# A hybrid decoder trunk: token halves for three pairs, seven products for eight

## The chip, the cores and the metric

The kernel runs on one core of a Trainium2 chip. The metric is the device time of one execution in microseconds. The engines are named as in the profile: PE (TensorE, matmuls), PEld (its weight loads), DVE (VectorE), ACT (ScalarE), POOL (GpSimd) and SP (SyncE, which here only issues DMAs).

## The reference

The input is x, 512 tokens of 1024 float32 values. Two layers follow, and a final RMSNorm. Layer 0 has a causal Conformer convolution and a SwiGLU FFN; layer 1 has sliding-window attention with its own query and output projections over one shared K/V, and a SwiGLU FFN. D_FF is 2816.

```python
def swiglu_ffn(x, w_up, w_down):
    gate, up = jnp.split(x @ w_up, 2, axis=-1)
    return (jax.nn.silu(gate) * up) @ w_down

def conformer_conv(x, w_pw1, b_pw1, w_dw, b_dw, ln_g, ln_b, w_pw2, b_pw2):
    a = jax.nn.glu(x @ w_pw1 + b_pw1, axis=-1)
    y = lax.conv_general_dilated(a, w_dw[:, None, :], ...) + b_dw
    y = jax.nn.silu(layernorm(y, ln_g, ln_b))
    return y @ w_pw2 + b_pw2
...
    for l in range(DEPTH):
        if l < N_A_LAYERS:
            h = h + conformer_conv(rmsnorm(h, norm_mix[l]), ...)
        else:
            ...
            h = h + attn @ w_o[j]
        h = h + swiglu_ffn(rmsnorm(h, norm_ffn[l]), ffn_w_up[l], ffn_w_down[l])
    return rmsnorm(h, norm_final)
```

## The kernel before

Everything lies transposed: h is [channels, tokens], 8 tiles of 128 channels by 512 tokens. Most matmuls keep float32 accuracy by splitting both operands into a high part (rounded to the fast format fp32r) and a low part (the rest): mm3 issues high × high, high × low and low × high (lines 380 to 382), the weights being the stationary operand. mm2 (lines 412 and 413) is the same for the second token half in the "twin" form, where one moving operand of 512 columns holds the high and the low part of 256 tokens side by side. A few chunks are multiplied as plain float32 (line 378).

The weights come as chunks of 512 KB, in the order of a list, PLAN. SP loads a chunk into one of six raw buffers, up to nine chunks ahead; ACT rounds it to the high part whi (L294), DVE subtracts to get the low part wlo (L297), each with four buffers and up to three chunks ahead of PE. The order of the instructions on every engine is fixed at build time by a scheduler, from the order of the code, and from rules of the kernel's own: issue_after (an instruction is not placed ahead of another), job and pace (background work is advanced at given chunk counts), and rate.

A "pair" is two 128-channel tiles of D_FF with gate and up; there are 11 pairs. In layer 0 the FFN treats them in two ways (HALVES0):

- Pairs 0 to 3 "by token halves": for the first half of the tokens (right after the first half of the convolution) four up chunks per pair, the gate, and two down chunks per pair, and later the same for the second half in the twin form.
- Pairs 4 to 10 "by seven products": the 2 × 2 block product of weights (channel blocks) and tokens (halves) is done with seven block products instead of eight, as in Strassen's scheme (SEVEN: A11 B11, S1 T1, S2 T2, A12 B21, S3 T3, S4 B22, A22 T4). S1 to S4 are sums of weight blocks. They are made in DRAM by DMAs: copy_sums has SP copy one block, and prepare() has POOL issue an accumulating DMA that adds the other (L289). share[0] is the number of such steps per weight chunk. T1 to T4 are sums of the tokens' rows, made by Rows0.sums.

The stages of layer 0, in the order of time: the convolution of the first token half; its second projection pw2 and the FFN of that half with pairs 0 to 3, with the convolution of the second half on DVE, ACT and POOL in the background (Half.background: the taps, then sums and scales for the LayerNorm, then spread and rows); the A12 products of pairs 4, 5 and 6, which need only tokens of the first half (FIRST); pw2 of the second half; the twin FFN of the second half; the seven products of pairs 4 to 10; their down chunks, at 512 columns.

The LayerNorm's last steps set when pw2 of the second half can start. spread is one matmul (L1089) that broadcasts mean and scale over the partitions; from it DVE makes the rows of z (L1101, L1102), ACT applies silu (L1103) and rounds (L544), and DVE subtracts for the low part (L545). In SevenPair.take, the bank of product A11 is read by DVE (L830) before product S2 writes into it; L840, L842, L849, L850 and L853 belong to the pair's other evacuations and its gate. The twin FFN's result goes through ACT (L604), DVE (L605), POOL (L606) and DVE (L607) into h.

Of the kernel before, what the change touches and what calls it, by code (L numbers as in the profile page):

```python
# [11 lines left out]
F32 = mybir.dt.float32  # L12
# [6 lines left out]
P = 128  # L19
# [12 lines left out]
EPS = 1e-6  # L32
NEG = -1e30
N_WARM = 6
HALVES0 = ((0, 4), (4, 11))
FIRST = (4, 5, 6)
LAST = FT // 2 - 1
STEPS1 = [("up", 0), ("up", 1), ("up", 2), ("low", 0)]
for _p in range(3, LAST, 2):
# [32 lines left out]
    return [(kind, pair, n.split()[0]) for n in SEVEN]  # L72


def part2_products():

    steps, held = [], []
    for pair in range(*HALVES0[1]):
        names = [n.split()[0] for n in SEVEN]
        if pair in FIRST:  # L80
            names = ["A11", "S1", "S2", "S4", "S3", "A22"]
        steps += [(pair, names[0])] + held
        held = [(pair, names.pop())] if pair in FIRST else []
        steps += [(pair, n) for n in names[1:]]
    return steps + held
# [6 lines left out]
def chunk_plan():  # L92
    plan = []

    def pw2():
        for g in range(2):
            for kp in range(KT // 2):
                plan.append(("pw2", kp, g))

    def downs(lo, hi):  # L100
        for g in range(2):
            for kp in range(lo, hi):
                plan.append(("down", 0, kp, g))
# [24 lines left out]
    return plan  # L128
# [81 lines left out]
def hybrid_trunk(ctx: ExitStack, tc: tile.TileContext, xT, W, prm_in, wdw_in, sinks, relb, onehot, fin, lead, out):  # L210
# [151 lines left out]
    def get(*key):  # L362
# [10 lines left out]
        sh = dict(a=n)  # L373
        return tuple(w and w.rearrange("p (a b) -> p a b", **sh) for w in (hi, lo))

    def mm3(out, w, x, start, stop, **kw):
        if w[1] is None:
            nc.tensor.matmul(out, w[0], x, start=start, stop=stop)  # L378
            return
        nc.tensor.matmul(out, w[0], x[0], start=start, stop=False, **kw)  # L380
        nc.tensor.matmul(out, w[0], x[1], start=False, stop=False, **kw)  # L381
        nc.tensor.matmul(out, w[1], x[0], start=False, stop=stop, **kw)  # L382

    class Act:
        def __init__(self, n, w=512):
# [177 lines left out]
    def down_group(keys, act_of, banks, on_step=None, on_m=None):  # L563
        nk = len(keys)
        w = banks[0].shape[-1]
        for ci, (key, kts) in enumerate(keys):
# [14 lines left out]
            if on_step is not None and on_m is None and ci == nk - 1:  # L581
                on_step()
                on_step()

    def ffn_part(layer, part, xg, tok, rms, on_h=None, twin=False, plain=None):
        lo, hi = HALVES0[part]
        hid = ffn_up(layer, lo, hi, xg, tok, rms, twin, plain)
        w = tok.stop - tok.start
        for g in range(2):
# [27 lines left out]
            if w == 256:  # L617
                rs_bc = rms.step2().unsqueeze(1).to_broadcast([P, 2, w])
                for e, b in enumerate(full):
                    i = g * 4 + 2 * e  # L620
                    nc.vector.tensor_mul(b, b, rs_bc)
                    nc.vector.tensor_add(hT[:, i:i + 2, tok], b, hT[:, i:i + 2, tok])
                    for k in range(2 if on_h is not None else 0):
                        on_h(i + k)
                continue
            for m in range(4):
                t = h[g * 4 + m][:, tok]
# [298 lines left out]
    def norm_x(rms, tok, pb=None):  # L926
# [4 lines left out]
                                           op0=ALU.mult, op1=ALU.mult)  # L931
        return pb

    with tc.tile_pool(name="conv", bufs=2) as cv:
        a_pad = [cv.tile([P, PAD + S], F32, tag=f"apad{ct}", name=uid("apad"), bufs=1) for ct in range(KT)]
        for a in a_pad:
# [39 lines left out]
        class Half:  # L976
# [131 lines left out]
            def background(self):  # L1108

                gen = self.conv()  # L1110
                due = []
                for p in range(KT // 2):
                    for s in range(TAPS - N_POOL[self.hf][p] + 1):
                        next(gen)
                        while due and due[0][0] <= s:
                            due.pop(0)[1]()
                        yield
                    due = [(10, self.shift_rows)] if p == 0 else []
                    due += [(11, lambda p=p: self.squares(p)), (12, lambda p=p: self.adds(p)), (15, lambda p=p: self.sums(p))]
# [132 lines left out]
        first = {pair: first[:, n, :].rearrange("p (a s) -> p a s", a=2) for n, pair in enumerate(FIRST)}  # L1252
        for pair in FIRST:
            pace()
            r = new_chain()
            product(("up0", pair, "A12"), [[x0["ffn0"][4 + k][e][:, HALF[0]] for k in range(4)] for e in range(2)], r, True)
            nc.scalar.copy(first[pair], r)
        flush()

# [12 lines left out]
    class Rows0:  # L1272
# [11 lines left out]
        def sums(self):  # L1284
# [6 lines left out]
            for n, (name, t, f, a, b) in enumerate((  # L1291
# [5 lines left out]
                if n == 3:  # L1297
# [6 lines left out]
                both = z0.tile([P, 2, 4, 256], F32R, tag="z0", name=uid("rows"), bufs=5)  # L1304
# [5 lines left out]
    z0 = part2.enter_context(tc.tile_pool(name="part2", bufs=5))  # L1310
    plain1 = z0.tile([P, KT, W2], F32, tag="z0", name=uid("plain1"), bufs=5)
# [12 lines left out]
    lo0, hi0 = HALVES0[1]  # L1324
    hid0, open_pairs = [], {}
    left = [n for n, _ in part2_products()]
    for pair, a in part2_products():
        if pair not in open_pairs:
            c = z0.tile([P, 2, 2, 2, 256], F32, tag="z0", name=uid("up"), bufs=5)
            open_pairs[pair] = SevenPair("up0", pair, rows0, c, first.get(pair))  # L1330
        open_pairs[pair].take(a)
        left.remove(pair)
        if pair in left:
            continue
        c = open_pairs[pair].gates()
        if 2 * (pair - lo0) == len(hid0):
            if pair == hi0 - 1:
                q = quad()
                two = q[:, 0:2], q[:, 2:4]
            else:  # L1340
                two = quad(), quad()
            hid0 += [[d[:, k, :] for d in two] for k in range(two[0].shape[1])]
        for m in range(2):
            split([d.rearrange("p (s q) -> p s q", s=2) for d in hid0[2 * (pair - lo0) + m]], c[:, m, :, 0, :])
    part2.close()

    attn = ExitStack()
    at = attn.enter_context(tc.tile_pool(name="attn", bufs=2))
    job(chain(*(read_bias(*b) for b in ((0, 0), (0, 1), (1, 0)))), (seen[0], 0), (seen[0] + 10, 7))
    share[0] = 0.6  # L1350
    if True:
# [346 lines left out]
```

## Time and profile before

| what | value |
|---|---|
| time, median of 3 runs | 1043.3 us (1042.69 to 1043.46) |
| the profiled execution | 1043.27 us, span 1041.5 us |
| granted TensorE clock | 0.997 |
| PE busy | 1031.5 us (99%), 6580 instructions |
| DVE busy | 776.5 us (75%) |
| ACT busy | 613.0 us (59%) |
| POOL busy | 473.2 us (45%) |
| DMA | 248.33 MB, mean 238 GB/s |

Matmuls are pipelined: a row's duration overlaps the next row's, and what a matmul costs PE is the step from its start to the start of the next. The stages before lie at these times of the span: pw2 of the first half from about 129 us, FFN of the first half 158 to 234, three A12 products 235 to 244, pw2 of the second half 244 to 267, twin FFN 267 to 335, seven products 335 to about 464, downs to about 540.

### The profile page before, as it was taken

Reading aid. Unit: us, or ns where it says so; the run is one execution under the profiler, and the core shown is the slowest. Engines: PE = TensorE matmul, PEld = TensorE weight load, DVE = VectorE, ACT = ScalarE, POOL = GpSimd, SP = SyncE. Lnnn points to the kernel's source line nnn. Section 1 sums busy time; section 2 is a strip of 40 time slices with the busy share of each in tenths; the row PEclk is TensorE's granted clock in tenths of the full one; section 3 lists DMA queues with packets and bytes.
Section 4 is the critical chain, followed back from the end, with each engine's and each line's share of the span. In section 5 each row is a group of like instructions: output and inputs, shape, how many; then the busy total and the mean of one; then the engine's idle time right before and its main releaser. Section 6 shows DMA issues by size and latency. Waiting matters only on the chain.

```text
span 1041.5 us, 17709 instructions
## 1 busy us (share of the span) xinstructions
PE 1031.5 (99%) x6580; PEld 932.6 (90%) x6580; DVE 776.5 (75%) x1202; ACT 613.0 (59%) x1062; POOL 473.2 (45%) x569
## 2 busy tenths in 40 slices
PE   9999999999999999999999999999999999999996
PEld 8888889999988999998888877788989999898995
DVE  3999989978789777673536566678686877868777
ACT  3887798847776556552333565466655556554654
POOL 3999999930535233221214255405442334434134
PEclk9999999999999999999999999999999999999998
DMA  9999747999999988999969766955879988877742
GB/s 356 340 315 207 205 126 204 272 256 275 249 239 262 304 220 284 256 301 244 286 209 254 210 183 183 228 154 152 252 230 312 287 264 264 245 233 222 224 150 81
DMA packets 67282, 248.33 MB, mean 238 GB/s; under 512 B 7579, under 2 KB 13884, under 8 KB 66364
## 3 DMA queue, kind: packets, MB, share of 16 engines
q1 hardware_dynamic: 54236, 200.75, 55.9%
q0 software_dynamic: 12672, 46.14, 24.8%
q8 instruction: 51, 0.84, 0.3%
q10 hardware_dynamic: 288, 0.31, 0.1%
q14 instruction: 35, 0.29, 0.1%
HBM read 241.93 MB, written 97.52 MB: 326 GB/s over the span
## 4 chain that ended last, share of the span: by engine, by line
PE 98%; DMA 0%; DVE 0%; issue 0%; POOLq 0%; SPq 0%; POOL 0%; ACT 0%
PE bank L380 20%; PE bank L382 20%; PE bank L381 20%; PE bank L960 10%; PE bank L902 9%; PE bank L412 4%; PE bank L378 4%; PE bank L413 2%; PE bank L1441 1%; PE bank L1483 1%; PE bank L1470 1%; PE bank L1058 1%; PE bank L1607 1%; PE bank L948 1%; DMA both<-in_lead_dram 0%; PE bank L1562 0%
## 5 line engine op out<-in xcount | busy, mean ns | idle before, releaser
L297 DVE TENSOR_TENSOR wlo<-raw,whi 128x1024 fp32r<-128x1024 f32 x246 | 329.7, 1348 | 136.8 <-ACT whi L294 136.5
L294 ACT CAST whi<-raw 128x1024 fp32r<-128x1024 f32 x246 | 257.1, 1049 | 276.6 <-PE bank L381 194.1
L380 PE MATMUL bank<-quad,whi 128*128 128x256 f32 (+1 forms) x976 | 307.4, 317 | 0.0
L381 PE MATMUL bank<-quad,whi 128*128 128x256 f32 (+1 forms) x976 | 306.6, 315 | 0.0
L382 PE MATMUL bank<-quad,wlo 128*128 128x256 f32 (+1 forms) x976 | 305.7, 315 | 0.0
L380 PEld LDWEIGHTS bank<-quad,whi 128*128 128x128 f32 x976 | 185.5, 191 | 12.8 <-issue 1.6
L381 PEld LDWEIGHTS bank<-quad,whi 128*128 128x128 f32 x976 | 186.0, 191 | 11.9 <-issue 0.5
L382 PEld LDWEIGHTS bank<-quad,wlo 128*128 128x128 f32 x976 | 185.6, 191 | 11.8 <-issue 0.4
L853 POOL TENSOR_TENSOR up<-up 128x512 f32<-128x512 f32 x34 | 62.9, 1851 | 283.6 <-ACT up L850 283.6
L1002 POOL TENSOR_TENSOR pr<-pr,pr 128x256 f32<-128x256 f32 x208 | 155.4, 788 | 2.6 <-ACT pr L1001 2.5
L380 PE MATMUL bank<-rows,whi 128*128 128x256 f32 x488 | 138.0, 283 | 0.0
L381 PE MATMUL bank<-rows,whi 128*128 128x256 f32 x488 | 137.8, 282 | 0.0
L382 PE MATMUL bank<-rows,wlo 128*128 128x256 f32 x488 | 137.8, 282 | 0.0
L1009 DVE SCALAR_TENSOR_TENSOR bank<-apad,wdw,bank 128x256 f32<-128x256 f32 x248 | 112.4, 485 | 3.4
L1001 ACT ACTIVATE pr<-apad,wdw 128x256 f32<-128x256 f32 x208 | 98.3, 502 | 14.9 <-POOL pr L1002 13.1
L960 PE MATMUL bank<-quad,w 128*128 128x256 f32 x448 | 98.7, 380 | 0.0
L960 PEld LDWEIGHTS bank<-quad,w 128*128 128x128 f32 x448 | 84.9, 190 | 11.8 <-DVE bank L1009 0.2
L380 PEld LDWEIGHTS bank<-rows,whi 128*128 128x128 f32 x488 | 93.1, 191 | 0.3
L381 PEld LDWEIGHTS bank<-rows,whi 128*128 128x128 f32 x488 | 93.1, 191 | 0.3
L382 PEld LDWEIGHTS bank<-rows,wlo 128*128 128x128 f32 x488 | 93.0, 191 | 0.0
L491 POOL TENSOR_TENSOR tmp<-tmp,tmp 128x256 f32<-128x256 f32 (+1 forms) x28 | 26.8, 957 | 101.4 <-ACT tmp L487 96.2
L412 PE MATMUL bank<-quad,whi 128*128 128x512 f32 x168 | 59.7, 398 | 0.0
(230 smaller groups left out, 1635.9 us busy)
## 6 DMA issues: line engine op xcount, KB each, us to landing
raw<-in_W_dram SPq DMA_DIRECT2D x170, 512.0 KB, 5.7
raw<-sum SPq DMA_DIRECT2D x88, 512.0 KB, 5.4
sum<-in_W_dram SPq DMA_DIRECT2D x52, 512.0 KB, 6.2
sum<-in_W_dram POOLq DMA_DIRECT2D x44, 512.0 KB, 9.6
sum<-sum POOLq DMA_DIRECT2D x44, 512.0 KB, 8.5
sum<-in_W_dram SPq DMA_DIRECT2D x4, 3584.0 KB, 30.4
w<-in_W_dram SPq DMA_DIRECT2D x14, 512.0 KB, 8.6
sum<-in_W_dram SPq DMA_DIRECT2D x4, 1024.0 KB, 30.3
```

What stands on the lines that cost most here:

```text
L294: on_act = nc.scalar.copy(hi, src).ins
L297: latest[:] = [on_act, lo_engine[0].tensor_sub(lo, src, f32(hi)).ins]
L380: nc.tensor.matmul(out, w[0], x[0], start=start, stop=False, **kw)
L381: nc.tensor.matmul(out, w[0], x[1], start=False, stop=False, **kw)
L382: nc.tensor.matmul(out, w[1], x[0], start=False, stop=stop, **kw)
L412: nc.tensor.matmul(first[2], first[0], first[1], start=start, stop=False)
L853: pool_op(nc.gpsimd.tensor_mul(gate, gate, c[:, m, :, 1, :]))
L902: nc.tensor.matmul(out, x, w[:, ws], start=first and e == 0 and i == 0, stop=e == 1 and i == 2, skip_group_check=True)
L960: mm = nc.tensor.matmul(self.pb[:, w * W2:(w + 1) * W2], w1_of(ct, w, k), x[k] if x else xg[k][:, tok], start=k == 0, stop=k == KT - 1)
L1001: on_act = nc.scalar.mul(pr, a[:, j:j + W2], tap(j))
L1002: on_pool = pool_op(nc.gpsimd.tensor_add(pr, acc, pr))
L1009: on_dve = nc.vector.scalar_tensor_tensor(yt if i == nd - 1 else c, src, tap(i), c if i else self.shift, op0=ALU.mult, op1=ALU.add)
```

## The change

Three pairs instead of four go by token halves (HALVES0), eight instead of seven by seven products, and these in two groups of four (GROUPS0): products of pairs 3 to 6, their down chunks, products of pairs 7 to 10, their down chunks. All eight pairs are in FIRST, so that all eight A12 products stand ahead of the second half's pw2; their results are kept in one quad and four new tiles (the pool keep). The addition of the first half's FFN into h is held back (held, let_go) and placed behind a given instruction of the convolution. The LayerNorm sums, scales and spread of the second half are placed behind the matmul that was last written (stamp). The convolution's job points, the pace points inside a product (between) and per take, and the shares of prepare() change: 0.45 to 0.5 in the first half, 0.25 to 0.45 in the groups, 0.6 in the last downs as before. The pool of rows and ups has four buffers instead of five, and odd pairs take a quad. In the built program the matmuls at 256 columns in the split form are 3804 instead of 3828, those at 512 columns remain 1518, and all others are the same.

PE around spread before (quad_1708 and quad_1709 are the hidden rows of a down chunk, quad_1395 the rows of the first A12 product, of which three whole ones follow):

```order
L381 MATMUL bank_2448<-quad_1709,whi_2485 128x256
L382 MATMUL bank_2448<-quad_1708,wlo_2486 128x256
L1089 MATMUL bank_2601<-tmp_2535,ones_m 128x512
L380 MATMUL bank_2611<-quad_1395,whi_2529 128x256
L381 MATMUL bank_2611<-quad_1395,whi_2529 128x256
L382 MATMUL bank_2611<-quad_1395,wlo_2530 128x256
```

And now (L384 to L386 are mm3's three matmuls, L1102 is spread, bank_2614 belongs to the seventh A12 product):

```order
L385 MATMUL bank_2614<-quad_1398,whi_2527 128x256
L386 MATMUL bank_2614<-quad_1398,wlo_2528 128x256
L1102 MATMUL bank_2633<-tmp_2572,ones_m 128x512
L384 MATMUL bank_2614<-quad_1398,whi_2527 128x256
L385 MATMUL bank_2614<-quad_1398,whi_2527 128x256
L386 MATMUL bank_2614<-quad_1398,wlo_2528 128x256
```

spread moved from ahead of all A12 products to the middle of the seventh of eight; 9 more matmuls of this one, the 24 of the eighth and then pw2 follow it.

DVE ahead of the reading of the first pair's A11 bank, before the change (bank_3755 is the A11 bank of pair 4, which S2 writes next):

```order
L297 TENSOR_TENSOR wlo_3759<-raw_3571,whi_3758 128x1024
L605 TENSOR_TENSOR tmp_3734<-bank_3636,tmp_3734 128x256
L605 TENSOR_TENSOR tmp_3739<-bank_3637,tmp_3739 128x256
L605 TENSOR_TENSOR tmp_3744<-bank_3638,tmp_3744 128x256
L605 TENSOR_TENSOR tmp_3749<-bank_3639,tmp_3749 128x256
L607 TENSOR_TENSOR h<-h,tmp_3734 128x256
L297 TENSOR_TENSOR wlo_3794<-raw_3594,whi_3793 128x1024
L607 TENSOR_TENSOR h<-h,tmp_3739 128x256
L607 TENSOR_TENSOR h<-h,tmp_3744 128x256
L830 TENSOR_TENSOR up_3754<-bank_3755,quad_2600 128x512
```

And now (bank_3578 is the A11 bank of pair 3; L299 is the weights' low part, L617 and L619 the twin result's additions, L1315 makes T4):

```order
L619 TENSOR_TENSOR h<-h,tmp_3467 128x256
L299 TENSOR_TENSOR wlo_3538<-raw_3349,whi_3537 128x1024
L619 TENSOR_TENSOR h<-h,tmp_3472 128x256
L619 TENSOR_TENSOR h<-h,tmp_3477 128x256
L299 TENSOR_TENSOR wlo_3582<-raw_3391,whi_3581 128x1024
L1315 TENSOR_TENSOR plain_1400<-plain_1400 128x1024
L617 TENSOR_TENSOR tmp_3557<-bank_3482,tmp_3557 128x256
L617 TENSOR_TENSOR tmp_3562<-bank_3483,tmp_3562 128x256
L617 TENSOR_TENSOR tmp_3567<-bank_3484,tmp_3567 128x256
L617 TENSOR_TENSOR tmp_3572<-bank_3485,tmp_3572 128x256
L299 TENSOR_TENSOR wlo_3615<-raw_3417,whi_3614 128x1024
L841 TENSOR_TENSOR up_3577<-bank_3578,quad_2381 128x512
```

Of the last four additions into h of the twin FFN, three stood ahead of that read before; now they stand behind it, and the sum of rows T4 has come ahead of it.

```diff
-HALVES0 = ((0, 4), (4, 11))
-FIRST = (4, 5, 6)
+HALVES0 = ((0, 3), (3, 11))
+GROUPS0 = ((3, 7), (7, 11))
+FIRST = tuple(range(3, 11))
...
-def part2_products():
+def part2_products(group):
...
-    for pair in range(*HALVES0[1]):
+    for pair in range(*group):
...
-    plan.extend(("up0", *step) for step in part2_products())
-    downs(*HALVES0[1])
+    for group in GROUPS0:
+        plan.extend(("up0", *step) for step in part2_products(group))
+        downs(*group)
...
+    stamp = [None]
+
     def mm3(out, w, x, start, stop, **kw):
...
-        nc.tensor.matmul(out, w[1], x[0], start=False, stop=stop, **kw)
+        stamp[0] = nc.tensor.matmul(out, w[1], x[0], start=False, stop=stop, **kw).ins
...
+    held = []
+
+    def let_go(behind):
+        b, rs_bc, into = held.pop(0)
+        with tc.issue_after(behind):
+            nc.vector.tensor_mul(b, b, rs_bc)
+            nc.vector.tensor_add(into, b, into)
...
-    def product(key, block, r, opens, closes=True):
+    def product(key, block, r, opens, between=None):
...
         for which in range(2):
+            if which and between is not None:
+                between()
...
                 for n, (_, f) in enumerate(due):
-                    f()
+                    with tc.issue_after(stamp[0]):
+                        f()
                     for _ in range((4, 1)[n]):
                         yield
-                self.scales_a()
+                with tc.issue_after(stamp[0]):
+                    self.scales_a()
...
-                self.spread()
+                with tc.issue_after(stamp[0]):
+                    self.spread()
                 yield from self.rows(True)
...
-        job(second, (base, 0), (base + 8, 19), (base + 13, 22), (base + 26, 40), (base + 30, 45), (base + 34, 50), (base + 35, h1.n_steps - early - 3))
+        job(second, (base, 0), (base + 8, 19), (base + 13, 22), (base + 26, 40), (base + 33, 43), (base + 34, 44), (base + 35, 44),
+            (base + 36, 45), (base + 37, 46), (base + 39, 48), (base + 40, 49), (base + 42, h1.n_steps - early))
...
-        preparing[0], share[0] = prepare(), 0.45
+        preparing[0], share[0] = prepare(), 0.5
...
-        first = quad(F32)
-        first = {pair: first[:, n, :].rearrange("p (a s) -> p a s", a=2) for n, pair in enumerate(FIRST)}
-        for pair in FIRST:
+        first = [quad(F32)] + [keep.tile([P, 512], F32, tag="c11", name=uid("c11")) for _ in FIRST[4:]]
+        first = {pair: t.rearrange("p (a s) -> p a s", a=2)
+                 for pair, t in zip(FIRST, [first[0][:, n, :] for n in range(4)] + first[1:])}
+        for n, pair in enumerate(FIRST):
             pace()
+            if n in (2, 3, 4, 5):
+                let_go(h1.last[1])
             r = new_chain()
-            product(("up0", pair, "A12"), [...], r, True)
+            product(("up0", pair, "A12"), [...], r, True, pace)
             nc.scalar.copy(first[pair], r)
...
-    job(rows0.sums(), (base + 11, 0), (base + 19, 8), (base + 26, 14), (base + 32, 17))
+    job(rows0.sums(), (base + 10, 0), (base + 16, 8), (base + 22, 12), (base + 27, 14), (base + 31, 17))
     pw2(h1.z, n1)
     ffn_part(0, 0, x0["ffn0"], HALF[1], n1.rms, twin=True)
-    flush()
...
-    share[0] = 1 / 4
-    lo0, hi0 = HALVES0[1]
...
+    share[0] = 0.45
+    for group in GROUPS0:
+        lo0, hi0 = group
+        last = hi0 == HALVES0[1][1]
...
+                if pair % 2:
+                    c = quads.tile([P, 2, 2, 2, 256], F32, tag="quad", name=uid("up"))
+                else:
+                    c = z0.tile([P, 2, 2, 2, 256], F32, tag="z0", name=uid("up"), bufs=4)
                 open_pairs[pair] = SevenPair("up0", pair, rows0, c, first.get(pair))
+            pace()
             open_pairs[pair].take(a)
...
         for g in range(2):
             banks = accs(512)
             down_group([(("down", 0, kp, g), 2 * (kp - lo0)) for kp in range(lo0, hi0)], lambda kt: hid0[kt], banks)
             for m in range(4):
                 nc.vector.tensor_add(h[g * 4 + m], banks[m], h[g * 4 + m])
-                nxt.on_h(g * 4 + m)
+                if last:
+                    nxt.on_h(g * 4 + m)
```

More of the change, by code (lines that the diff above doesn't have):

```diff
@@ L374, in get @@
         return tuple(w and w.rearrange("p (a b) -> p a b", **sh) for w in (hi, lo))
+    stamp = [None]
     def mm3(out, w, x, start, stop, **kw):
         if w[1] is None:
-            nc.tensor.matmul(out, w[0], x, start=start, stop=stop)
+            stamp[0] = nc.tensor.matmul(out, w[0], x, start=start, stop=stop).ins
             return
@@ L619, in ffn_part @@
                 for e, b in enumerate(full):
[L620 to L624, printed above, removed]
+                    into = hT[:, g * 4 + 2 * e:g * 4 + 2 * e + 2, tok]
+                    held.append((b, rs_bc, into))
                 continue
@@ L932, in norm_x @@
         return pb
+    kept = ExitStack()
+    keep = kept.enter_context(tc.tile_pool(name="keep", bufs=max(1, len(FIRST) - 4)))
     with tc.tile_pool(name="conv", bufs=2) as cv:
@@ L1303, in sums @@
                     return
-                both = z0.tile([P, 2, 4, 256], F32R, tag="z0", name=uid("rows"), bufs=5)
+                both = z0.tile([P, 2, 4, 256], F32R, tag="z0", name=uid("rows"), bufs=4)
                 self.block[name] = [[both[:, e, k] for k in range(4)] for e in range(2)]
@@ L1309, in hybrid_trunk @@
     part2 = ExitStack()
[L1310 to L1311 removed]
+    z0 = part2.enter_context(tc.tile_pool(name="part2", bufs=4))
+    plain1 = z0.tile([P, KT, W2], F32, tag="z0", name=uid("plain1"), bufs=4)
     n1 = Next(("ffn0",), x0, bc0, HALF[1])
@@ L1315, in hybrid_trunk @@
     rows0.rms = rows0
-    job(rows0.sums(), (base + 11, 0), (base + 19, 8), (base + 26, 14), (base + 32, 17))
+    job(rows0.sums(), (base + 10, 0), (base + 16, 8), (base + 22, 12), (base + 27, 14), (base + 31, 17))
     pw2(h1.z, n1)
     ffn_part(0, 0, x0["ffn0"], HALF[1], n1.rms, twin=True)
-    flush()
     nxt = Next(("kv", "mix1"))
-    share[0] = 1 / 4
-    lo0, hi0 = HALVES0[1]
[L1325 to L1351, printed above, removed]
+    share[0] = 0.45
+    for group in GROUPS0:
+        lo0, hi0 = group
+        last = hi0 == HALVES0[1][1]
+        hid0, open_pairs = [], {}
+        left = [n for n, _ in part2_products(group)]
+        for pair, a in part2_products(group):
+            if pair not in open_pairs:
+                if pair % 2:
+                    c = quads.tile([P, 2, 2, 2, 256], F32, tag="quad", name=uid("up"))
+                else:
+                    c = z0.tile([P, 2, 2, 2, 256], F32, tag="z0", name=uid("up"), bufs=4)
+                open_pairs[pair] = SevenPair("up0", pair, rows0, c, first.get(pair))
+            pace()
+            open_pairs[pair].take(a)
+            left.remove(pair)
+            if pair in left:
+                continue
+            c = open_pairs[pair].gates()
+            if 2 * (pair - lo0) == len(hid0):
+                if pair == hi0 - 1:
+                    q = quad()
+                    two = q[:, 0:2], q[:, 2:4]
+                else:
+                    two = quad(), quad()
+                hid0 += [[d[:, k, :] for d in two] for k in range(two[0].shape[1])]
+            for m in range(2):
+                split([d.rearrange("p (s q) -> p s q", s=2) for d in hid0[2 * (pair - lo0) + m]], c[:, m, :, 0, :])
+        flush()
+        if last:
+            part2.close()
+            kept.close()
+            attn = ExitStack()
+            at = attn.enter_context(tc.tile_pool(name="attn", bufs=2))
+            job(chain(*(read_bias(*b) for b in ((0, 0), (0, 1), (1, 0)))), (seen[0], 0), (seen[0] + 7, 7))
+            share[0] = 0.6
@@ L1356, in hybrid_trunk @@
                 nc.vector.tensor_add(h[g * 4 + m], banks[m], h[g * 4 + m])
-                nxt.on_h(g * 4 + m)
+                if last:
+                    nxt.on_h(g * 4 + m)
+    if True:
         x, rms = nxt.x, nxt.rms
```

2 lines of the change are left out of this document (1 added, 1 removed).

## The prediction

> **What bounds the kernel now.** I read the page first, then the waits of PE, the timeline around the two places the change disturbs, and last the DMA queues.
>
> ```profile
> span 1041.5 us, 17709 instructions
> PE 1031.5 (99%) x6580; PEld 932.6 (90%) x6580; DVE 776.5 (75%) x1202; ACT 613.0 (59%) x1062; POOL 473.2 (45%) x569
> PE 98%; DMA 0%; DVE 0%; issue 0%; POOLq 0%; SPq 0%; POOL 0%; ACT 0%
> ```
> ```profile
> PE bank L465 <- POOL ones_m L462: 1.1, 1, 1.1
> PE bank L948 <- DVE quad L922: 0.7, 2, 0.4
> ```
>
> PE is busy for 99% of the span, the chain that ended last is 98% PE, and the second fence (all that PE ever waited for another engine) holds 1.8 us, both of it at the start. So the time is the sum of the steps at which PE issues matmuls. An edit is worth the steps it saves, less every stall it opens; PE never waits today, so a stall of any length is paid in full. ACT (59%) and DVE (75%) have room on average, which says nothing about a place where a result is wanted soon.
>
> The steps, as start to start on the PE timeline (the second number of a row is a pipelined duration and is not additive):
>
> ```profile
> 339.50 0.28 PE L380 MATMUL bank<-rows,whi 128*128 128x256 f32 x1
> ...
> 340.93 0.28 PE L380 MATMUL bank<-rows,whi 128*128 128x256 f32 x1
> ```
> ```profile
> 300.35 0.40 PE L412 MATMUL bank<-quad,whi 128*128 128x512 f32 x1
> ...
> 302.12 0.40 PE L412 MATMUL bank<-quad,whi 128*128 128x512 f32 x1
> ```
> ```profile
> 500.35 0.39 PE L380 MATMUL bank<-quad,whi 128*128 128x512 f32 x1
> ...
> 502.84 0.39 PE L382 MATMUL bank<-quad,wlo 128*128 128x512 f32 x1
> ```
>
> Twelve 256-column steps lie between the first two rows: 1.43/12 = 0.119 us. Five pairs of the twin form (L412 with 512 columns, L413 with 256) lie between the next two: 1.77/5 = 0.354 us a pair. Eleven 512-column steps lie between the last two: 2.49/11 = 0.226 us.
>
> **The sum on PE.** Pair 3 moves from token halves to seven products. Removed: in token half 0, 4 up and 2 down chunks of 24 matmuls, 144 × 0.119 = 17.1 us; in half 1 the same 6 chunks in twin form, 8 pairs each, 48 × 0.354 = 17.0 us. Added: 7 products of 24 matmuls, 168 × 0.119 = 20.0 us; 2 down chunks of 24 at 512 columns, 48 × 0.226 = 10.8 us. Net 30.8 - 34.1 = -3.3 us. Splitting the seven products in two groups adds no matmul, since each pair keeps its two down chunks; it costs 8 more DVE additions to h (0.68 each, the L830 row below has that shape), 5.4 us in all beside the downs of the first group and the products after them, where DVE is 74% busy at most (96.04 of 129 us in the window row below). Moving five A12 products ahead of the second projection costs PE nothing by itself.
>
> **First place: the second projection (pw2 of half 1).** Its operands come from spread, the matmul L1089 (L1102 in the changed code) that broadcasts the LayerNorm factors: DVE subtracts and multiplies, ACT takes silu, ACT casts the high part, DVE the low part, eight rows of z in all. The part on the change shows the order: before, three whole A12 products (72 matmuls) follow spread; now spread stands inside the seventh A12 product. Behind it are 9 matmuls of that product and 24 of the eighth, and then pw2. So 33 matmuls cover the chain from spread to z, where 72 did.
>
> ```profile
> 234.28 1.02 PE L1089 MATMUL bank<-tmp,ones_m 128*128 128x512 f32 x2
> 243.76 0.40 PE L380 MATMUL bank<-quad,whi 128*128 128x256 f32 x2
> ```
> ```profile
> 239.04 1.09 ACT L1103 ACTIVATE tmp<-tmp,prm 128x256 f32<-128x256 f32 x2
> 240.03 0.70 ACT L544 CAST quad<-tmp 128x256 fp32r<-128x256 f32 x2
> 240.64 0.57 ACT L1257 COPY quad<-bank 128x512 f32<-128x512 f32 x1
> 241.11 1.05 ACT L294 CAST whi<-raw 128x1024 fp32r<-128x1024 f32 x1
> ```
> ```profile
> 240.33 0.41 DVE L1102 TENSOR_TENSOR tmp<-tmp,bank 128x256 f32<-128x256 f32 x1
> 240.66 0.41 DVE L1101 TENSOR_TENSOR tmp<-y,bank 128x256 f32<-128x256 f32 x1
> 240.99 0.76 DVE L545 TENSOR_TENSOR quad<-tmp,quad 128x256 fp32r<-128x256 f32 x2
> 242.32 1.22 DVE L297 TENSOR_TENSOR wlo<-raw,whi 128x1024 fp32r<-128x1024 f32 x1
> ```
>
> Before: spread's result is there at 234.28 + 1.02 = 235.30, pw2 starts at 243.76, so 8.46 us of cover. After: the cover is 9.48 - 39 × 0.119 = 4.84 us from spread's start, 3.8 us from its result. Count t from that result. On ACT the cast of a weight chunk (1.05, next start after 0.96) waits for a buffer that the nine matmuls free at about 0.95; then come the copy of an A12 bank (0.47 to the next), two silus (0.50 each), and the cast of z row 0, ready at 0.95 + 0.96 + 0.47 + 1.0 + 0.40 = 3.8: just in time. Its low part (L545) stands on DVE behind the low part of that weight chunk (L297, 2.05 to 3.2), a multiply and a subtract (0.33 each), so it runs 3.85 to 4.25, and the third matmul of pw2 wants it at 3.8 + 0.24 = 4.05: late by 0.3 with the release. Rows are used 12 matmuls (1.43 us) each, so row 2 is wanted at 3.8 + 2.86 + 0.3 = 6.95. ACT's next weight cast (4.0 to 5.05) and copy, three silus and the cast make it 7.3: late by 0.4. Its low part stands behind the next L297 and two more operations and is ready at 8.1, wanted at 7.6: late by 0.5. Rows 3 to 7 then have over a microsecond. Sum **1.2 us** (0.3 if only row 0 is late; 2.0 if each ACT and DVE step is a tenth longer, which moves all three).
>
> **Second place: the start of the seven products.** The third product of the first pair (S2) writes into the bank of the first, so it waits until DVE has read that bank (L830, L841 after).
>
> ```profile
> 327.44 0.37 ACT L604 COPY tmp<-bank 128x256 f32<-128x256 f32 x1 [0.32 <-PE bank L413]
> ```
> ```profile
> 335.38 4.01 POOL L606 TENSOR_TENSOR tmp<-tmp,rsbc 128x256 f32<-128x256 f32 x4 [2.83 <-DVE tmp L605]
> ```
> ```profile
> 334.88 1.40 DVE L605 TENSOR_TENSOR tmp<-bank,tmp 128x256 f32<-128x256 f32 x4
> 336.21 0.89 DVE L607 TENSOR_TENSOR h<-h,tmp 128x256 f32<-128x256 f32 x1
> 337.02 1.76 DVE L297 TENSOR_TENSOR wlo<-raw,whi 128x1024 fp32r<-128x1024 f32 x1
> 338.71 1.29 DVE L607 TENSOR_TENSOR h<-h,tmp 128x256 f32<-128x256 f32 x2
> 339.93 0.68 DVE L830 TENSOR_TENSOR up<-bank,quad 128x512 f32<-128x512 f32 x1
> 340.86 1.21 DVE L297 TENSOR_TENSOR wlo<-raw,whi 128x1024 fp32r<-128x1024 f32 x1
> ```
>
> L830 ends at 340.61 and S2 starts at 340.93: 0.32 us of slack. DVE has no gap there. From the copy of the last bank of the first down group (327.44) to S2 it has 13.5 us. The change's part shows what DVE has there now (L299 is L297, L617 and L619 are L605 and L607, L1315 makes a sum of rows). Between the same two points PE now has only 10 twin pairs and two products: 3.5 + 5.7 = 9.3 us. DVE's work: copy and first add 0.8, L619 three times 0.55, three L299 at 1.69, 1.14 and 1.69 (the dear ones beside POOL's multiplies: 1.76 against 1.21 us in the rows), L1315 of the same shape 1.13, four L617 1.33, L841 0.68: 10.1 us. Late by **0.7** us (0 if the first L299 escapes POOL and the adds pack; 1.2 if all three meet it). The Trainium skill, SBUF — State Buffer, Who interferes with whom, says that the port DVE and GpSimd share is an exclusive lock, so that an operation with two SBUF inputs blocks until GpSimd's is over. By that each L299 would lose up to a whole POOL multiply, about 1.0 us instead of the 0.5 the rows show, and the place would cost 1.4; the row decides here.
>
> **Elsewhere.** Ends of both groups: from the copy of the A22 bank (L842) to the low part of the pair's hidden rows (L545) it takes 364.41 - 357.87 = 6.5 us:
>
> ```profile
> 357.87 0.59 ACT L842 ACTIVATE up<-bank 128x512 f32<-128x512 f32 x1
> ```
> ```profile
> 363.73 0.68 DVE L545 TENSOR_TENSOR quad<-up,quad 128x512 fp32r<-128x512 f32 x1
> ```
>
> Between the last A22 and the first use of that pair's rows PE has rather more than a down chunk and a half of other pairs, 1.6 × 24 × 0.226 = 8.7 us; I put it at nothing, with 1 us of lateness as the bound if a cast comes in between. The twin stage has one pair less and the same work for a pair; nothing.
>
> **DMA.** The share of prepared sums in the groups rises from 0.25 to 0.45.
>
> ```profile
> 335.00:464.00 129.00, 129.00 (x1083) 128.95 (x1082) 96.04 (x110) 72.44 (x95) 37.45 (x28) 1.00 0.92 266
> ```
> ```profile
> q1 hardware_dynamic: 6714, 27.32, 60.1%
> q0 software_dynamic: 1895, 6.89, 31.2%
> ...
> raw<-in_W_dram SPq DMA_DIRECT2D x23, 512.0 KB, 7.7
> ```
>
> The DMA engines are at 0.92 in the seven products already (the queues' lines are of the same window). A load or copy of SP costs 0.601 × 129/54 = 1.44 us of all engines, an accumulation of POOL 0.312 × 129/13 = 3.1. The second group's 24 products (69 us) come with 24 loads, 11 copies and 10 accumulations: 35 × 1.44 + 10 × 3.1 = 81 us, 12 more than there are. Loads land in 7.7 us; six raw buffers let one be issued six products (17 us) ahead, and casts run up to three chunks ahead of PE. 7.7 + 12 = 19.7 exceeds 17 by 3, inside those three chunks (8.6 us). I put it at nothing.
>
> **Sum.** 1043.27 (profiled execution, 0.03 under the median of 1043.3) - 3.3 + 1.2 + 0.7 = 1041.9; about **1042.0** against the median. Changes under 0.2% (2.1 us) are what I call the same; this is -0.13%.
>
> **Rivals.**
> 1. Everything is covered, 1043.3 - 3.3 = 1040.0, or up to 1041.2 with one of the places open. For it: no place is late by more than 0.7 at a time, and my DVE steps include POOL's interference. Against: three lots of lateness at pw2 that each follow from rows. 0.28.
> 2. Slower: DMA falls behind in the second group. If the POOL queue takes its half of the engines, as it does at 48% in a window before this one, SP's 50 us of loads and copies get 35 of 69: loads slip 16 us, 7.7 + 16 = 24, less 17 + 5.7 (two chunks of casts) leaves 1 to 2; each further accumulation that lands late adds 3.1, and the first group, which is at 0.96 by the same count, hands on its own lag of some 3. That is 4 to 8 us of stall, 1046 to 1050. It decides from a landing time of about 23 us. Against: a share of 0.95 was carried before at landings of 6 to 8. 0.27. The Trainium skill's page DMA: Bandwidth & Descriptors (Specifications) gives HBM some 358 GB/s for a core. Counting a copy and an accumulation as a read and a write, the second group moves 24 + 2 × 21 times 0.52 MB in 69 us, 500 GB/s, and by that rule it would end far later, above 1055; this trace shows 266 GB/s moved (about 310 so counted) and nothing near that limit, so it stands for a part of this chance only.
>
> Beside these stands the forecast, with pw2 and the start costing 1 to 3 us: 1041.2 to 1043.5, 0.45.
>
> **How the numbers follow.** The forecast is the likeliest case, 1042.0, its own range 1041.2 to 1043.5. Leaving out the deepest part of rival 1 and the far part of rival 2 gives 1040.0 to 1047.0. Faster by over 0.2% (below 1041.2): rival 1, 0.28 and a sliver of the forecast, 0.30. Slower by over 0.2% (above 1045.4): rival 2, 0.27. Same: 0.43.
>
> **What the next profile would show.** PE waits on DVE and ACT in pw2, 0.3, 0.4 and 0.5 us, on rows 0 and 2 of z; a PE wait of 0.7 on DVE L841 before the third product; loads landing later in the second group, with no PE wait on a cast. The sum on PE holds if PE's span less its waits falls by 3.3. I am wrong if waits on a cast (L296) show in the second group, if pw2's waits come to over 3 us, or if a wait stands at a place I gave nothing.

## The result, and the profile after

| | before | changed |
|---|---|---|
| time, median of 4 runs | 1043.07 us (1042.69 to 1043.46) | 1048.7 us (1047.73 to 1049.12) |
| ratio to before | | 1.0053 (95% interval 1.0035 to 1.0070) |
| span of the profiled execution | 1041.5 us | 1047.3 us |

The changed kernel is 0.5% slower, outside the predicted range and on the other side of the forecast. The page after, its first lines and the chain that ended last:

```profile
span 1047.3 us, 17675 instructions
PE 1031.3 (98%) x6556; PEld 931.1 (89%) x6556; DVE 783.3 (75%) x1208; ACT 611.0 (58%) x1059; POOL 480.2 (46%) x573
PE 78%; DVE 10%; ACT 4%; issue 3%; DMA 2%; POOL 2%; SPq 0%; POOLq 0%; DVEq 0%; ACTq 0%
```

PE has 24 matmuls fewer, but the chain, which was 98% PE, now leads through DVE, ACT and POOL for 16% of the span. The waits of PE (engine and line, the releaser, then us in total, times, longest):

```profile
PE bank L386 <- DVE wlo L299: 2.2, 1, 2.2
PE bank L533 <- ACT tmp L519: 1.5, 1, 1.5
PE bank L384 <- ACT whi L296: 1.1, 1, 1.1
PE bank L469 <- POOL ones_m L466: 1.1, 1, 1.1
PE bank L384 <- ACT quad L548: 0.8, 1, 0.8
PE bank L961 <- DVE quad L933: 0.8, 1, 0.8
PE bank L385 <- DVE quad L549: 0.3, 1, 0.3
```

L469 and L961 are the two waits at the start that the kernel before has too. The other five are new. On the PE timeline, with the releaser in brackets:

```profile
182.32 0.28 PE L386 MATMUL bank<-quad,wlo 128*128 128x256 f32 x1
184.08 0.70 PE L533 MATMUL bank<-tmp,ones_m 128*128 128x256 f32 x2 [1.48 <-ACT tmp L519]
...
202.00 0.28 PE L385 MATMUL bank<-quad,whi 128*128 128x256 f32 x1
204.46 0.39 PE L386 MATMUL bank<-quad,wlo 128*128 128x256 f32 x1 [2.18 <-DVE wlo L299]
...
207.08 0.28 PE L386 MATMUL bank<-quad,wlo 128*128 128x256 f32 x1
208.20 0.50 PE L384 MATMUL bank<-quad,whi 128*128 128x256 f32 x2 [0.84 <-ACT quad L548]
```

These three stand in the FFN of the first token half, a stage for which the prediction had no term. Start to start, less one step of 0.12 us each, they cost 5.0 us (1.64 + 2.34 + 1.00), and the step right behind each is 0.1 us longer than usual: 5.3 us in all. On DVE and on POOL at the second of them:

```profile
198.70 5.71 DVE L299 TENSOR_TENSOR wlo<-raw,whi 128x1024 fp32r<-128x1024 f32 x1
```
```profile
198.35 0.78 POOL L291 DMA_DIRECT2D sum<-in_W_dram  x1
198.92 4.39 POOL L1015 TENSOR_TENSOR pr<-pr,pr 128x256 f32<-128x256 f32 x6
203.05 1.02 POOL L291 DMA_DIRECT2D sum<-sum  x1
```

The subtraction that makes a low part takes 1.21 us when nothing disturbs it; here it takes 5.71, and it ends a little after POOL's six multiplies and the DMA issue behind them do. The multiplies stand 0.69 us apart and all follow an accumulating DMA. The third stall follows from the second: the gate product (L671) whose cast PE waits for stands behind the late subtraction on DVE. The first stall has the same picture at 172 us, with two DMA issues ahead and a subtraction of 5.51 us (the second of the two in the DVE row):

```profile
171.32 1.87 POOL L291 DMA_DIRECT2D sum<-in_W_dram  x2
172.60 2.04 POOL L1026 TENSOR_TENSOR y<-y,pr 128x256 f32<-128x256 f32 x2
173.99 2.03 POOL L1015 TENSOR_TENSOR pr<-pr,pr 128x256 f32<-128x256 f32 x2
```
```profile
170.71 7.19 DVE L299 TENSOR_TENSOR wlo<-raw,whi 128x1024 fp32r<-128x1024 f32 x2
```
```profile
170.31 1.02 POOL L289 DMA_DIRECT2D sum<-in_W_dram  x1
171.06 2.74 POOL L1013 TENSOR_TENSOR y<-y,pr 128x256 f32<-128x256 f32 x2
173.74 0.81 POOL L289 DMA_DIRECT2D sum<-in_W_dram  x1
```

The first two fences are the changed kernel, the third the one before. Until there every engine's instructions are the same in both programs; the first that differs anywhere is this second DMA, which the share of 0.5 instead of 0.45 puts ahead of the y additions.

### The profile page after: what moved, and what is told of

The parts are those of the page before. It is cut to its first block, busy times and chain, and to the rows that moved or that the text cites. A ratio compares the mean times of both kernels' runs of the same rounds, so it can differ in the third digit from the quotient of the medians.

```text
span 1047.3 us, 17675 instructions
## 1 busy us (share of the span) xinstructions
PE 1031.3 (98%) x6556; PEld 931.1 (89%) x6556; DVE 783.3 (75%) x1208; ACT 611.0 (58%) x1059; POOL 480.2 (46%) x573
## 4 chain that ended last, share of the span: by engine, by line
PE 78%; DVE 10%; ACT 4%; issue 3%; DMA 2%; POOL 2%; SPq 0%; POOLq 0%; DVEq 0%; ACTq 0%
PE bank L384 19%; PE bank L385 19%; PE bank L386 19%; PE bank L913 9%; DVE bank L1022 6%; PE bank L416 3%; PE bank L417 2%; ACT pr L1014 2%; POOL pr L1015 2%; DVE wlo L299 2%; PE bank L1469 1%; PE bank L1511 1%; PE bank L1498 1%; DMA w<-in_W_dram 1%; PE bank L1635 1%
## 5 line engine op out<-in xcount | busy, mean ns | idle before, releaser
L299 DVE TENSOR_TENSOR wlo<-raw,whi 128x1024 fp32r<-128x1024 f32 x243 | 323.5, 1338 | 133.3 <-ACT whi L296 132.9
L296 ACT CAST whi<-raw 128x1024 fp32r<-128x1024 f32 x243 | 253.9, 1048 | 278.3 <-PE bank L385 198.7
L384 PE MATMUL bank<-quad,whi 128*128 128x256 f32 (+1 forms) x976 | 308.5, 319 | 1.0 <-ACT quad L548 0.8
L386 PE MATMUL bank<-quad,wlo 128*128 128x256 f32 (+1 forms) x976 | 306.0, 316 | 2.2 <-DVE wlo L299 2.2
L864 POOL TENSOR_TENSOR up<-up 128x512 f32<-128x512 f32 x36 | 68.0, 1890 | 320.6 <-ACT up L861 320.6
L384 PEld LDWEIGHTS bank<-quad,whi 128*128 128x128 f32 x976 | 185.3, 190 | 15.1 <-issue 1.6
L386 PEld LDWEIGHTS bank<-quad,wlo 128*128 128x128 f32 x976 | 185.3, 190 | 14.8 <-DVE wlo L299 2.4
L384 PE MATMUL bank<-rows,whi 128*128 128x256 f32 x512 | 144.8, 283 | 1.1 <-ACT whi L296 1.1
L386 PE MATMUL bank<-rows,wlo 128*128 128x256 f32 x512 | 144.6, 282 | 0.0
L385 PE MATMUL bank<-rows,whi 128*128 128x256 f32 x512 | 144.6, 282 | 0.0
L384 PEld LDWEIGHTS bank<-rows,whi 128*128 128x128 f32 x512 | 97.6, 191 | 1.6 <-ACT whi L296 1.3
L385 PEld LDWEIGHTS bank<-rows,whi 128*128 128x128 f32 x512 | 97.6, 191 | 0.3
L386 PEld LDWEIGHTS bank<-rows,wlo 128*128 128x128 f32 x512 | 97.6, 191 | 0.0
L913 PE MATMUL bank<-wlo,fhi 128*128 128x512 f32 x140 | 55.2, 394 | 0.0
```

The costliest lines, as they stand in the source:

```text
L296: on_act = nc.scalar.copy(hi, src).ins
L299: latest[:] = [on_act, lo_engine[0].tensor_sub(lo, src, f32(hi)).ins]
L386: stamp[0] = nc.tensor.matmul(out, w[1], x[0], start=False, stop=stop, **kw).ins
L864: pool_op(nc.gpsimd.tensor_mul(gate, gate, c[:, m, :, 1, :]))
L913: nc.tensor.matmul(out, x, w[:, ws], start=first and e == 0 and i == 0, stop=e == 1 and i == 2, skip_group_check=True)
```

## The experiments

The experiments ran on three chips (x1 to x4 on one, x5 to x8 on the second, x9 on the third), on which the kernel before took 1044.7, 1045.1 and 1044.9 us, more than the 1043.1 us above. So the ratios to the kernel before on the same chip are what compares; a difference in microseconds holds only within a chip. All experiments are short edits, and some stand on top of earlier ones. Traces of the kernel before and of the changed kernel exist only from the first measurement.

**Is it the share of prepared sums, or the three pairs?** Two crossed edits. The first takes the share back in the changed kernel:

```diff
-        preparing[0], share[0] = prepare(), 0.5
+        preparing[0], share[0] = prepare(), 0.45
```

> The changed kernel with the share of prepared sums in the first half back at 0.45. Up to the end of that stage the order on POOL is then word for word that of the kernel before. Theory (one accumulating DMA placed ahead of POOL's multiplies lets a DVE low-part subtraction stand blocked for 5.5 us, and PE waits): no DVE subtraction over 3.5 us between 150 and 225 us, no PE wait there, and 1048.7 - 5.1 = 1043.6 us. Rival (the stage is slow because one pair less leaves DVE and POOL less PE time for the same convolution): the waits stay, 1048.7 us.

Measured: 1045.36 us, ratio 1.0008 (0.9999 to 1.0017), instead of 1.0053. The wait of 1.5 us is gone, the 2.2 us became 1.0, the 0.8 stayed at 0.9, and the time is 1.8 us above the 1043.6 that the theory gave. The second edit puts 0.5 into the kernel before:

```diff
-        preparing[0], share[0] = prepare(), 0.45
+        preparing[0], share[0] = prepare(), 0.5
```

> The kernel before with nothing changed but the share in the first half, 0.45 to 0.5. Theory: the same two blocked DVE subtractions of 5 to 6 us and PE waits of 3.5 to 5.1 us, so 1046.5 to 1048.2 us. Rival (the three pairs and the new order make the waits): 1043.1 us, no PE wait.

Measured: 1049.23 us, ratio 1.0043 (1.0028 to 1.0058). This one number makes the kernel before as slow as the changed one, and its list of PE waits shows the same two:

```profile
PE bank L382 <- DVE wlo L297: 2.2, 1, 2.2
PE bank L529 <- ACT tmp L515: 1.3, 1, 1.3
```

The third wait of the changed kernel is not in x2. In its place the granted clock falls to 0.52 from 203.0 to 206.5 us, and 16 matmuls take steps of 0.21 us instead of 0.12, which costs 1.5 us; why the clock fell there is open.

So the theory holds for most of the loss and the rival (one pair less) does not explain it. It held only in part for the changed kernel: 1.9 us of waits remain at 200 and 204 us with the share at 0.45, where the trace of the kernel before has none. One subtraction of 4.35 us is left at 197 us. Yet up to there every engine's instructions are the same in x1 and in the kernel before. Six multiplies behind a DMA issue, and the subtraction that starts 1.18 us after the first of them, in the kernel before and in x1:

```profile
194.95 6.49 POOL L1002 TENSOR_TENSOR pr<-pr,pr 128x256 f32<-128x256 f32 x6
196.13 1.61 DVE L297 TENSOR_TENSOR wlo<-raw,whi 128x1024 fp32r<-128x1024 f32 x1
```
```profile
195.67 4.43 POOL L1015 TENSOR_TENSOR pr<-pr,pr 128x256 f32<-128x256 f32 x6
196.85 4.35 DVE L299 TENSOR_TENSOR wlo<-raw,whi 128x1024 fp32r<-128x1024 f32 x1
```

In the first POOL waits in between and DVE gets through, in the second DVE stands. So at this place the order of the instructions does not decide; what does is open.

**Is it the accumulating DMAs?** The changed kernel without them in that stage:

```diff
             with tc.issue_after(pooled[0]):
+              if not quiet[0]:
                 nc.gpsimd.dma_start(summed[c], chunk(c, SUMS[c[2]][1]), accum_op=ALU.add, max_dma_last_dim=4096)
...
+        quiet[0] = False
         first = [quad(F32)] + ...
```

> The changed kernel without the accumulating DMAs of POOL while the first token half's FFN runs (the sums due there are left as plain copies; all else stays). Theory that a run of multiplies behind an accumulating DMA blocks DVE: without the DMAs no subtraction over 2 us between 150 and 225 us, no PE wait there, some 1043.5 us. Rival (POOL's multiplies alone block DVE): subtractions of 3 us and more and PE waits remain.

Measured: 1043.16 us in a single execution (the kernel before 1044.66). No PE wait is left in the stage. All subtractions between 150 and 230 us, count and min/median/max in ns, in the changed kernel and in this one:

```profile
L299 DVE TENSOR_TENSOR wlo<-raw,whi x20: 1209/1218/5710, 164.2 to 228.3; 128x1024 fp32r<-128x1024 f32 x20
```
```profile
L302 DVE TENSOR_TENSOR wlo<-raw,whi x22: 1214/1292/1820, 163.5 to 229.2; 128x1024 fp32r<-128x1024 f32 x22
```

The longest falls from 5.71 to 1.82 us, while POOL still does all its multiplies. The rival, that the multiplies alone block DVE, falls as far as one trace can show it.

**The place of a DMA, or their rate?** The changed kernel at 0.5, its count of steps begun half a step lower:

```diff
-        preparing[0], share[0] = prepare(), 0.5
+        preparing[0], share[:] = prepare(), [0.5, -0.5]
```

> The changed kernel (share 0.5) with the count of steps started half a step lower, so that the same rate puts each accumulating DMA a chunk later; one DMA stands ahead of the two y additions on POOL at 172 us instead of two. Theory (the place of a DMA ahead of ready POOL work decides, not the rate): the blocked subtraction of 5.5 us at 172 us and the PE wait of 1.6 us behind it vanish, 1.6 us or more under the changed kernel. Rival (the rate of 0.5 itself is too high): still 5 us over x1_share45.

Measured: median 1043.84 us, ratio 0.9995 (0.9985 to 1.0005): all 5 to 6 us are back at an unchanged rate. PE's longest wait in the stage is 0.16 us; a subtraction of 3.97 us remains at 205 us that nobody waits for. Nor is it the load of the DMA engines: from 160 to 185 us, where the first stall stood, their mean share is 0.74 in the changed kernel and 0.77 here. Its ten runs reach from 1042.94 to 1048.26 us, wider than any other kernel's here. Why one of them was as slow as the changed kernel is open, as only one execution has a trace.

A second place says the same in all eleven traces. In layer 1, near 710 us, POOL makes sums of 128x1024 elements one behind the other. Where the issue of an accumulating DMA stands between the first and the second (the kernel before, x1, x2, x4, x6, x8), DVE's subtraction beside them takes 8.05 to 8.07 us; where none does (the changed kernel, x3, x5, x7, x9), 2.68 to 2.69. PE waits for it in none. The kernel before, and the changed one:

```profile
705.00 0.82 POOL L289 DMA_DIRECT2D sum<-sum  x1
705.57 2.67 POOL L759 TENSOR_TENSOR quad<-quad,t 128x1024 f32<-128x1024 f32 x1
707.93 5.01 POOL L759 TENSOR_TENSOR quad<-quad,quad 128x1024 f32<-128x1024 f32 x2
705.96 8.07 DVE L297 TENSOR_TENSOR wlo<-raw,whi 128x1024 fp32r<-128x1024 f32 x1 [3.44 <-ACT whi L294]
```
```profile
711.04 2.42 POOL L768 TENSOR_TENSOR quad<-quad,t 128x1024 f32<-128x1024 f32 x1
713.41 6.73 POOL L768 TENSOR_TENSOR quad<-quad,quad 128x1024 f32<-128x1024 f32 x2
711.85 2.69 DVE L299 TENSOR_TENSOR wlo<-raw,whi 128x1024 fp32r<-128x1024 f32 x1 [3.45 <-ACT whi L296]
```

**The second projection.** On top of x1, the points of the LayerNorm's last steps three chunk counts earlier, so that 72 matmuls stand behind spread, as before:

```diff
-        job(second, (base, 0), ..., (base + 33, 43), (base + 34, 44), (base + 35, 44),
-            (base + 36, 45), (base + 37, 46), (base + 39, 48), (base + 40, 49), (base + 42, h1.n_steps - early))
+        job(second, (base, 0), ..., (base + 30, 43), (base + 31, 44), (base + 32, 44),
+            (base + 33, 45), (base + 34, 46), (base + 36, 48), (base + 37, 49), (base + 39, h1.n_steps - early))
```

> As x1_share45, and the job points of the LayerNorm statistics, scales and spread of the second half three chunk counts earlier, so that 72 matmuls instead of 33 stand between spread and the second projection. Theory (the cover behind spread is 4.7 us too short by 1.26 us): the waits in the second projection vanish and the time is 1.2 us under x1_share45, 1042.4 us. Rival (the statistics come before their inputs are ready, and the wait moves to them): as x1_share45 or slower, with a PE wait on the statistics' inputs.

Measured: 1044.36 us, 1.0 us under x1, ratio 0.9995 (0.9985 to 1.0005). The wait on L549 is gone and no wait has come at the statistics. The theory holds.

**The sums out of that stage.** On top of x4, with the computation whole:

```diff
-        preparing[0], share[0] = prepare(), 0.45
         ffn_part(0, 0, x0["ffn0"], HALF[0], n0.rms, plain=plain)
+        preparing[0], share[0] = prepare(), 0.5
         first = [quad(F32)] + ...
...
-            share[0] = 0.6
+            share[0] = 0.8
```

> As x4_spread_early, but the prepared sums begin only with the A12 products (share 0 instead of 0.45 in the first half's FFN, then 0.5; 0.8 instead of 0.6 in the last downs of layer 0). The computation is whole. Theory (accumulating DMAs among the convolution's multiplies on POOL block DVE): the two PE waits of 1.0 and 0.9 us that x4 has at 200 and 204 us vanish, 2.1 us under x4, 1042.3 us beside a kernel before of 1044.7. Rival (sums that come later make DMA the bound in the groups): PE waits on casts or a late load appear after 330 us, no gain.

Measured: 1041.62 us, ratio 0.9969 (0.9958 to 0.9980); x4's was 0.9995, so some 2.7 us less. The longest subtraction in the stage is 1.82 us, as in x7 and x9, which keep this edit. Both waits are gone, and no new wait on a cast or load has come in the groups, though their sums come later.

**The start of the seven products.** Two edits on DVE's queue. First, on top of x4, T4 later:

```diff
-    job(rows0.sums(), ..., (base + 27, 14), (base + 31, 17))
+    job(rows0.sums(), ..., (base + 27, 14), (base + 31, 14), (base + 33, 17))
```

> As x4_spread_early, with the sum of rows T4 (1.13 us of DVE) behind the reading of the first pair's A11 bank; one addition of 0.6 us comes ahead of it instead. Theory (the wait before the third product, 1.26 us, is DVE's queue): it shrinks by 0.5 us, 1043.9 us. Rival (the wait is for the cast on ACT that the list of waits names): it stays at 1.26 us, 1044.4 us.

Measured: 1043.76 us, ratio 0.9987 (0.9978 to 0.9997), which overlaps x4's interval. The wait before the third product shrank from 1.1 to 0.9 us in the list of waits, and it is now put down to the reading of the bank:

```profile
PE bank L384 <- DVE up L841: 0.9, 1, 0.9
```

By the trace the gain at that place is 0.25 us, half of what was expected, because the addition L619 that came ahead of the reading took 0.95 us beside POOL, not 0.6. Both together:

> x5_no_share_first and x6_t4_late together: if both theories hold and add, 1044.4 - 2.1 - 0.5 = 1041.8 us, 0.28% under the kernel before on the same chip.

Measured: 1041.92 us, ratio 0.9970 (0.9959 to 0.9981). It is no faster than x5 alone beyond the intervals. Last, on top of x7, one weight subtraction behind the reading:

```diff
-                    nc.vector.tensor_add(c11, r, self.early)
+                    add = nc.vector.tensor_add(c11, r, self.early).ins
+                    if self.pair == FIRST[0]:
+                        biased[0] = add
             elif a == "S1":
+                biased[0] = None
```

> As x7_both, with the low part of one weight chunk placed behind the reading of the first pair's A11 bank on DVE. Theory (the last wait on PE, 1.0 us before the third product, is DVE's queue ahead of that reading, 1.7 us of it this subtraction): the wait is gone and no other takes its place, 1.0 us under x7_both, ratio to the kernel before 0.996. Rival (the subtraction that is late now holds the fourth product): a PE wait on it of some 1 us, ratio 0.997.

Measured: 1040.2 us, ratio 0.9957 (0.9943 to 0.9971). The interval overlaps x7's; the trace shows the 1.1 us that this place still lost in x7 gone. What is left of PE's waits is the start:

```profile
PE bank L469 <- POOL ones_m L466: 1.0, 1, 1.0
PE bank L964 <- DVE quad L936: 0.3, 1, 0.3
```

This kernel does the changed kernel's matmuls without its waits and beats both: it takes 4.7 us less than the kernel before on the same chip.

## Why the prediction was wrong

**The sum on PE, -3.3 us: right.** x9 has the same matmuls and no wait but the start. From PE's hundredth matmul to its last the trace of the kernel before takes 1033.05 - 23.96 = 1009.1 us and that of x9 1030.02 - 24.11 = 1005.9, 3.2 us less. The 4.7 us by which x9's median lies under the kernel before on its own chip are 1.5 more. There is no trace of the kernel before from there, so where those 1.5 us lie is open; that it loses time there where x1 does is possible and not shown.

**The second projection, +1.2 us: right.** From its first matmul to the first of row 4 of z:

```profile
247.35 0.50 PE L384 MATMUL bank<-quad,whi 128*128 128x256 f32 x2
...
254.35 0.28 PE L384 MATMUL bank<-quad,whi 128*128 128x256 f32 x1
```

7.00 us for 48 matmuls that take 48 × 0.1197 = 5.75: 1.25 us lost, and 1.0 us came back in x4. The list of waits names 0.3 us of it only.

**The start of the seven products, +0.7 us: right place and cause, too small.** The third product came 1.28 us late (1.40 from 328.65 to 330.05, less one step). The list of waits puts it down to a cast (L296), but the reading ends 0.14 us ahead of the matmul, and it was reordering DVE that removed the wait in x9:

```profile
319.81 0.38 ACT L616 COPY tmp<-bank 128x256 f32<-128x256 f32 x1 [0.38 <-PE bank L417]
```
```profile
328.65 0.28 PE L386 MATMUL bank<-rows,wlo 128*128 128x256 f32 x1
330.05 0.36 PE L384 MATMUL bank<-rows,whi 128*128 128x256 f32 x1 [1.12 <-ACT whi L296]
```
```profile
329.23 0.68 DVE L841 TENSOR_TENSOR up<-bank,quad 128x512 f32<-128x512 f32 x1
```

DVE's 10.1 us from the copy of the last bank to the end of the reading came out as forecast (319.81 to 329.91). PE's side was too long: without the stall it is there after 9.0 us, not 9.3, and the prediction had no term for the 0.14 us from the reading to the matmul. Besides, 10.1 - 9.3 is 0.8 and not 0.7.

**DMA in the groups, nothing: right.** The window with the second group holds 13 copies and 8 accumulations in 80 us; the kernel before moves as many in the 129 us of its products. PE waits for nothing there:

```profile
440.00:520.00 80.00, 80.00 (x615) 77.45 (x614) 54.86 (x62) 41.96 (x54) 24.40 (x19) 1.00 0.94 303
```

The rival that made DMA the bound ended on the right side for the wrong reason. The Trainium skill, DMA: Bandwidth & Descriptors, Specifications, has some 358 GB/s of HBM for a core. In this window 303 GB/s are moved; with the 13 copies and 8 accumulations of 0.52 MB counted twice, (24.23 + 11.0) MB in 80 us are an estimated 440 GB/s, and no wait shows. The measurement decides.

**The step that failed** is "Elsewhere": it looked at the ends of the groups and the twin stage, and nowhere in the sum stands the rise of the share from 0.45 to 0.5 in the first token half. The diff has it, and the working under DMA took up only the groups. One of the prediction's own signs of being wrong, a wait at a place that was given nothing, is what came. There the cost is 5.3 us of stalls on PE, which come from POOL's queue and not from DMA bandwidth. How much of it is the share's has two parts. The first stall follows the place of one accumulating DMA that the share puts a step earlier: it is there in the changed kernel and x2, and in no run at 0.45 or with the steps shifted. The second and third came at 0.45 too (x1, x4, x6), the second at half its size and the third at its full size, so for them it is shown only that accumulating DMAs must be in the stage (they are gone in x3, x5, x7 and x9), not that the share of 0.5 makes them.

With the forecast of 1042.0, the 5.3 us, the 0.6 by which the second place was too small and the 0.2 by which the sum on PE was too large (3.1 by the steps of both traces) give 1048.1. The profiled execution of 1049.1 has another 1.0 us at its start, with the same instructions in both kernels up to there: PE's hundredth matmul starts at 24.98 us after and 23.96 before, and at 23.34 in x2. So it does not come from the change.

The price of DVE beside POOL also failed, at the point where a rule was weighed. The prediction took from the rows that a subtraction loses 0.5 us beside POOL's multiplies and set that against the Trainium skill's exclusive lock (SBUF — State Buffer, Who interferes with whom), by which it would lose up to a whole POOL operation. The runs show a third thing: behind a DMA issue a subtraction can stand through six multiplies, 5.71 - 1.21 = 4.5 us. That is more than one lock's worth; without the DMAs the worst in that stage is 1.82 - 1.21 = 0.6, under the 0.69 us of one multiply, which agrees with the lock of one operation.

## What to carry to other kernels

When PE has no gap, go through every edit of a diff, each constant too, and ask on every queue what moves: a number that sets how often something is issued moves every instruction of that queue. Make the list from the order of both programs, engine by engine, and start at the first instruction that differs: here it was a DMA issue with a stall right behind it. And keep DMA issues on POOL out of stretches in which POOL has ready work and DVE has subtractions that PE waits for.

## What the runs showed of the hardware

A DVE operation with two SBUF inputs, 1.21 us alone, took 3.4 to 5.7 us when it started in a run of POOL operations that stood ready behind the issue of an accumulating DMA, and at most 1.82 us in the same stage without those DMAs (x3, x5, x7, x9). At the place near 710 us it took 8.05 us and more behind such an issue and 2.69 at most without one. The issue makes it possible and not certain: in the kernel before a subtraction in such a run took 1.61 us. Why POOL does not let DVE in between in such a run, and does otherwise, no run here tells.

The list of waits understates and misnames short stalls: it gave 0.3 us for a place that lost 1.25, and an ACT cast for a wait that ended with a DVE operation. Start to start on the PE timeline is what adds up.
